# A decoder trunk of two layers: the first FFN begins on half of its first channel block, and layer 0's scale and gate come in groups of 512 channels

## The chip, the core and the metric

The kernel runs on one NeuronCore of a Trainium2 chip. The metric is the device time of one execution in microseconds (us). The engines are PE (matmul), with PEld for its weight loads, DVE (vector), ACT (scalar), POOL and SP; SP issues nearly all the DMA loads here.

## The reference

One sequence of 256 tokens and 2048 channels passes two layers in float32. Layer 0 mixes by causal pooling over 2, 4, 8 and 16 tokens in four channel groups of 512, layer 1 by latent attention; each has a SwiGLU FFN of 5632 channels behind its mixer. A condition vector c gives, by one large matrix, shift, scale and gate for each part. The change touches layer 0 up to the start of its FFN:

```python
sc = silu(c)
shift_m, scale_m, gate_m, shift_f, scale_f, gate_f = split(sc @ mod_w[0] + mod_b[0], 6)   # 2048 x 12288
h = rmsnorm(x, norm_mix) * (1 + scale_m) + shift_m
y = pool_mixer(h, pool_w, pool_scale)     # per group g of 512 channels: window means - h, then @ pool_w[g]
x = x + gate_m * y
h = rmsnorm(x, norm_ffn) * (1 + scale_f) + shift_f
x = x + gate_f * ((silu(h @ w_gate) * (h @ w_up)) @ w_down)
```

## The kernel before

**Work and precision.** FFN products are made as three passes of rounded float32: a weight tile `raw` is split into an upper part (ACT) and a lower part (DVE), and so is the activation; a block of 512 x 512 weights for 256 tokens is 24 matmuls of 128x512 (line 422 at the helper `proj_unit`). The four 512-channel blocks of the FFN's input are called j = 0 to 3. `start_ffn` takes six of the eleven chunks of 512 hidden channels (`begun`), gate and up, through j = 0, 1, 2 before the normal FFN code goes on.

**The opening** is written in a fixed order (`manual_schedule`): each engine carries out its instructions as the program lists them. A list `units` names one load of 1 MB each, and `then(n, f)` hangs other work behind unit n. Loads use six buffers (`raw`), so SP issues a load when a buffer has come free.

- `shift`, `scale`, `gate`, 16 units each, and `block`, 8 units, are `Strips`: PE multiplies each loaded tile by a column of silu(c), four narrow products (line 258), and sums in one bank. At the end `columns` copies the bank (ACT and DVE, 264 and 265), and PE turns it (269) into columns of one value a channel. `block` holds the FFN's shift and scale for j = 0.
- Seven tiles of `gate` are summed on DVE instead (241, 243).
- `Part` (213) is the other way to sum, used for the later background loads: DVE multiplies a tile of the transposed matrix by a row of silu(c) and sums along it.
- For each group g: `pool_half` (two halves: transposes 1029 and window means 1022, 1023, 1034, 1035 on PE), `pool_modulate` (four scaled shift rows on ACT, 1046, then four operations on DVE, 1048), `pool_product` (four steps of four matmuls, 1059; copy on ACT, 1062), `mix_in` (gate and residual on DVE, 1069; squares on ACT, 1073 and 1076; their sum on DVE, 1077), `turn_back` (transposes 1102, copies 1103).
- At the end: `norm_sums` (1089), a power on POOL, `norm_spread` (1110, copied at 1111), `hidden_T` (1121), and `halves_T` (1134, 1138, 1144), which gives the FFN's first input. The first FFN weights are `Halved`: two loads of half a MB.

Of the kernel before, what the change touches and what calls it, by code (L numbers as in the profile page):

```python
# [50 lines left out]
C_PAIR = C_SEL + NSTRIP  # L51
C_SHORT = C_PAIR + 2
# [8 lines left out]
TURNED_BY_DMA = (range(6, 9), range(10))  # L61

# [13 lines left out]
def shape_constants():  # L76
# [8 lines left out]
    for i in range(NSTRIP):  # L85
        con[i * STRIP, C_SEL + i] = 1.0
        con[i * STRIP, C_PAIR + i % 2] = 1.0

# [7 lines left out]
def tile_trunk(ctx: ExitStack, tc: tile.TileContext, a: dict, out: bass.AP):  # L96
# [50 lines left out]
    def load_ahead():  # L147
        kt = len(ahead)
        ahead.append(raw_t([P, 1, NSTRIP, CH]))
        sync.dma_start(ahead[kt].rearrange("p k i n -> p (k i n)"), a["mod_w"][0, kt * P:(kt + 1) * P, :D])  # L150
# [21 lines left out]
    one_strip = const.tile([P, STRIP], F32, name="one_strip")  # L172
# [6 lines left out]
    pool.memset(one_strip, 0.0)  # L179
    pool.memset(one_strip[:, 0:1], 1.0)  # L180
# [40 lines left out]
    class Strips:  # L221
        def __init__(self, i, pair, done, aside=()):
            self.aside, self.acc, self.bank = aside, None, None
            self.n, self.rows, self.done, self.kt = (2, 2, done, 0) if pair else (NSTRIP, 1, done, 0)
            self.w = a["mod_block"] if pair else a["mod_w"][0][:, i * D:(i + 1) * D].rearrange("(k p) n -> k p n", p=P)
# [9 lines left out]
        def use(self, r):  # L235
            last = self.kt + self.rows == KD
            if self.kt in self.aside:
                s_ = s_col[:, self.kt:self.kt + 1]
                if self.acc is None:
                    self.acc = gate_t([P, 1, NSTRIP, CH])  # L240
                    dve.tensor_scalar(out=self.acc, in0=r, scalar1=s_, scalar2=None, op0=ALU.mult)
                else:
                    dve.scalar_tensor_tensor(out=self.acc, in0=r, scalar=s_, in1=self.acc, op0=ALU.mult, op1=ALU.add)
            else:
                self.sum(lambda k: s_strip[:, self.kt + k, :], r, last and self.acc is None)
            if last and self.acc is not None:
                self.sum(lambda k: one_strip, self.acc, True)
            self.kt += self.rows
            if self.kt == KD:
                self.done(self.columns())  # L250

        def sum(self, weights, r, last):
            first = self.bank is None
            if first:
                self.bank = ps_t()
            for m in range(NSTRIP):
                k, i = m // self.n, m % self.n
                pe.matmul(self.bank[m * STRIP:(m + 1) * STRIP, :], lhsT=weights(k), rhs=r[:, k, i, :], start=first, stop=last)  # L258

        def columns(self):  # L260
# [5 lines left out]
            pick = con[:, C_SEL:C_SEL + NSTRIP] if self.rows == 1 else con[:, C_PAIR:C_PAIR + 2]  # L266
# [125 lines left out]
    class Halved:  # L392


        def __init__(self, src):
            shape = [P, KL, CH]
            self.src, self.raw, self.hi, self.lo = src, raw_t(shape), hl_t(shape), hl_t(shape)
            early[repr(src)] = self.hi, self.lo

        def load(self, h):  # L400
            ks = slice(h * KL // 2, (h + 1) * KL // 2)
            sync.dma_start(self.raw[:, ks].rearrange("p k n -> p (k n)"), self.src[:, ks.start * CH:ks.stop * CH])

        def upper(self, h):
            ks = slice(h * KL // 2, (h + 1) * KL // 2)
            act.activation(self.hi[:, ks], self.raw[:, ks], AF.Copy)

        def lower(self, h):
            ks = slice(h * KL // 2, (h + 1) * KL // 2)
# [1393 lines left out]
```

## Time and profile before

| | us |
|---|---|
| median of 3 runs | 1886.86 (1886.29 to 1887.82) |
| profiled execution | 1886.89 |
| its span | 1885.1 |
| PE busy | 1836.3 |
| DVE busy | 1434.9 |
| ACT busy | 836.4 |

The profiled execution stands 1.79 us above its span, which lies around the work that the profile covers. Its mean granted clock was 0.989. PE is busy at 90% or more in all slices of 47 us but the first three and the last, and a PE that is busy in the profile is not always at its peak. The DMA engines moved 592 MB, and in the first six slices they were busy all the time.

### The profile page before, as it was taken

What the parts mean: (1) busy time and instruction counts of PE and PEld (TensorE: products, weight loads), DVE (VectorE), ACT (ScalarE), POOL (GpSimd) and SP (SyncE); (2) the same over time, 40 slices, a digit from 0 to 9 for tenths busy, and PEclk for the clock granted to TensorE, in tenths of its full rate; (3) what the DMA queues carried; (4) which work ended last, traced back from release to release, by engine and by line L of the source; (5) the groups of instructions that cost most, each with busy time, mean ns of one, the idle gap of its engine ahead of it and who ended that gap; (6) DMA issues with size and microseconds to landing.
All of it is one profiled execution on the core that took longest, in us unless ns stands there. A gap on an engine that the chain in (4) does not pass through costs nothing.

```text
span 1885.1 us, 21743 instructions
## 1 busy us (share of the span) xinstructions
PE 1836.3 (97%) x8605; PEld 1488.5 (79%) x8605; DVE 1434.9 (76%) x1443; ACT 836.4 (44%) x914; POOL 68.1 (4%) x100
## 2 busy tenths in 40 slices
PE   6689999999999999999999999999999999999998
PEld 2356888888888888888889888888888888888886
DVE  1247799999889798997798886889897666645557
ACT  3125643444433344244766645643454433343343
POOL 0000000000000000000100000100011000000000
PEclk8889999999999999999999999999999999999999
DMA  9999998889999899995594485999798676776651
GB/s 399 415 420 413 386 368 331 320 313 366 407 352 419 350 403 393 386 420 217 188 379 171 160 353 189 407 358 356 279 343 320 261 261 243 260 261 234 222 201 45
DMA packets 85335, 592.27 MB, mean 314 GB/s; under 512 B 10049, under 2 KB 10481, under 8 KB 16497
## 3 DMA queue, kind: packets, MB, share of 16 engines
q1 hardware_dynamic: 79346, 570.68, 77.9%
q0 software_dynamic: 5648, 19.93, 2.9%
q8 instruction: 67, 1.10, 0.2%
q10 hardware_dynamic: 240, 0.29, 0.0%
q14 instruction: 34, 0.28, 0.0%
HBM read 576.15 MB, written 14.70 MB: 313 GB/s over the span
## 4 chain that ended last, share of the span: by engine, by line
PE 94%; DMA 5%; DVE 0%; ACT 0%; SPq 0%; issue 0%; POOLq 0%; DVEq 0%; ACTq 0%
PE ps L422 80%; DMA raw<-in_mod_w_dram 4%; PE ps L431 2%; PE ps L1059 2%; PE ps L258 2%; PE ps L1412 1%; PE ps L1498 1%; PE ps L1604 1%; PE ps L1315 1%; PE ps L807 0%; DMA raw<-in_mod_block_dram 0%; PE ps L1501 0%; PE ps L198 0%; PE ps L1513 0%; PE ps L1553 0%; PE ps L1514 0%
## 5 line engine op out<-in xcount | busy, mean ns | idle before, releaser
L422 PE MATMUL ps<-hl,act 128*128 128x512 f32 x6672 | 1517.7, 390 | 0.0
L422 PEld LDWEIGHTS ps<-hl,act 128*128 128x128 f32 x6672 | 1251.3, 188 | 259.6 <-ACT act L1134 0.8
L376 ACT ACTIVATE hl<-raw 128x2048 fp32r<-128x2048 f32 x285 | 545.9, 1918 | 631.7 <-PE ps L422 413.4
L378 DVE TENSOR_TENSOR hl<-raw,hl 128x2048 fp32r<-128x2048 f32 x285 | 651.8, 2288 | 203.6 <-ACT hl L376 203.2
L213 DVE SCALAR_TENSOR_TENSOR raw<-raw,s_row 128x2048 f32<-128x2048 f32 x168 | 383.4, 2286 | 9.9 <-DMA raw<-in_mod_wt_dram 9.9
L258 PE MATMUL ps<-raw,s_strip 128*32 128x512 f32 x392 | 59.6, 699 | 35.1 <-DMA raw<-in_mod_w_dram 34.3
L755 DVE TENSOR_TENSOR act<-ps,act 128x512 f32<-128x512 f32 x96 | 64.2, 685 | 10.3 <-PE ps L422 10.2
L258 PEld LDWEIGHTS ps<-raw,s_strip 128*32 128x32 f32 x392 | 9.2, 117 | 64.5 <-DMA raw<-in_mod_w_dram 41.6
L431 PE MATMUL ps<-hl,act 128*128 128x512 f32 x192 | 47.7, 401 | 0.6 <-DVE act L527 0.5
L431 PEld LDWEIGHTS ps<-hl,act 128*128 128x128 f32 x192 | 35.1, 188 | 10.3 <-ACT act L514 2.5
L575 POOL DMA_DIRECT2D turned<-t2k x32 | 17.8, 555 | 637.6 <-DVE t2k L573 637.4
L820 DVE TENSOR_TENSOR x<-ps,x 128x512 f32<-128x512 f32 x32 | 21.7, 691 | 20.8 <-PE ps L422 20.8
L544 DVE TENSOR_TENSOR hl<-raw,hl 128x2048 fp32r<-128x2048 f32 (+3 forms) x17 | 31.9, 1879 | 4.8 <-ACT hl L541 4.7
L265 DVE COPY t2k<-ps 128x256 f32<-128x256 f32 x4 | 1.7, 425 | 42.6 <-ACT t2k L264 42.6
L1059 PEld LDWEIGHTS ps<-act,act 128*128 128x128 f32 x128 | 24.5, 198 | 11.5 <-issue 8.4
L882 ACT ACTIVATE t2k<-ps 128x512 f32<-128x512 f32 x24 | 14.2, 592 | 42.8 <-PE ps L422 42.6
L451 ACT ACTIVATE junk<-x 128x512 bf16<-128x512 f32 x23 | 14.5, 628 | 42.1 <-DVE x L669 24.9
L753 ACT ACTIVATE act<-ps 128x512 f32<-128x512 f32 x32 | 19.0, 594 | 29.4 <-PE ps L422 29.4
L886 DVE TENSOR_TENSOR t2k<-ps,t2k 128x512 f32<-128x512 f32 x24 | 16.5, 686 | 20.1 <-PE ps L422 20.1
L1059 PE MATMUL ps<-act,act 128*128 128x256 f32 x128 | 31.7, 400 | 0.0
L541 ACT ACTIVATE hl<-raw 128x2048 fp32r<-128x2048 f32 (+1 forms) x15 | 26.5, 1766 | 3.5 <-PE ps L422 3.5
L1024 DVE COPY hl<-ps 128x256 f32<-128x256 f32 x4 | 1.7, 423 | 32.3 <-PE ps L1023 32.3
(239 smaller groups left out, 1057.2 us busy)
## 6 DMA issues: line engine op xcount, KB each, us to landing
raw<-in_mod_wt_dram SPq DMA_DIRECT2D x136, 1024.0 KB, 6.8
raw<-in_ffn_up_dram SPq DMA_DIRECT2D x88, 1024.0 KB, 6.4
raw<-in_ffn_down_dram SPq DMA_DIRECT2D x88, 1024.0 KB, 6.5
raw<-in_ffn_gate_dram SPq DMA_DIRECT2D x87, 1024.0 KB, 6.5
raw<-in_mod_w_dram SPq DMA_DIRECT2D x48, 1024.0 KB, 13.6
raw<-in_kv_mod_wt_dram SPq DMA_DIRECT2D x32, 1024.0 KB, 9.3
raw<-in_w_o_dram SPq DMA_DIRECT2D x16, 1024.0 KB, 6.6
raw<-in_mod_block_dram SPq DMA_DIRECT2D x8, 1024.0 KB, 12.5
```

Of the source, the lines that this page charges most:

```text
L213: dve.scalar_tensor_tensor(out=r, in0=r, scalar=1.0, in1=s_row, op0=ALU.mult, op1=ALU.mult, accum_out=self.sums[:, self.n:self.n + 1])
L258: pe.matmul(self.bank[m * STRIP:(m + 1) * STRIP, :], lhsT=weights(k), rhs=r[:, k, i, :], start=first, stop=last)
L376: hi_ins = act.activation(hi, r, AF.Copy)
L378: lo_ins = dve.tensor_tensor(out=lo, in0=r, in1=hi.bitcast(F32), op=ALU.subtract)
L422: pe.matmul(banks[tok], lhsT=t_[:, i, k, tok * P:(tok + 1) * P], rhs=w[:, k, :], start=first and n < len(part), stop=last and n >= len(ord ...
L431: pe.matmul(bank, lhsT=t_[:, i, k, tok * P:(tok + 1) * P], rhs=w[:, k, :], start=first and n == 0, stop=last and n == len(order) - 1)
L541: hid_ins[0] = act.activation(w[1], w[0], AF.Copy)
L544: dve.tensor_tensor(out=w[2][:, ks], in0=w[0][:, ks], in1=w[1][:, ks].bitcast(F32), op=ALU.subtract)
L753: act.activation(part, banks[tok], AF.Copy)
L755: dve.tensor_tensor(out=part, in0=banks[tok], in1=part, op=ALU.add)
L820: dve.tensor_tensor(out=sums, in0=bank, in1=sums, op=ALU.add)
L1059: pe.matmul(mixed[g][:, n % 2, :], lhsT=wp[g][:, k, ns], rhs=pool_all[g // 2][:, g % 2, k, :], start=k == 0, stop=k == KL - 1)
```

## The change

Four things are changed in the opening.

1. `scale` (called AM) and `gate` (GM) are loaded by groups of 512 channels, four units a group. Of the eight groups four stay on PE as `Strips` (`BY_PE`: scale 0 and 2, gate 0 and 3), with tiles cut by group; the other four are `Part` on DVE. The sums aside on DVE are gone.
2. Each group's pool work follows its own scale group, and its `mix_in` its own gate group. `mix_in` adds each square to the sum at once; the squares of the last group go to PE as sums of their own.
3. `block` holds the FFN's shift and scale of 256 channels only, four units. Those of the other 256 (`upper_block`) are four `Part` tiles after the first products.
4. The first two chunks of the FFN, gate and up, take j = 0 in two halves of 256 channels (`Pair`, `HalfBlock`), each load of 1 MB with gate and up side by side. The first halves of both pairs are loaded inside the last gate group. In `start_ffn` these two chunks are left out at j = 0, and the background loads begin one block later.

```diff
+AM, GM = 1, 2
+BY_PE = ((AM, 0), (AM, 2), (GM, 0), (GM, 3))
+PAIRS = 2
...
+    def group_of(m, g):
+        kt = slice(g * KL, (g + 1) * KL)
+        dst, factor = scales[m]
+        if (m, g) in BY_PE:
+            return Strips(a["mod_groups"][BY_PE.index((m, g))], 1, lambda v: add_bias(dst, v[:, 0, :], m, kt, factor))
+        return Part(a["mod_wt"][0], range(m * KD + kt.start, m * KD + kt.stop),
+                    lambda sums: add_bias(dst, sums, m, kt, factor))
...
+    block = Strips(a["mod_block"], 1, lambda v: block_cols(v[:, 0, :], 0))
+    upper_block = Part(a["mod_wt"][0], [i * KD + k for i in (3, 4) for k in range(KL // 2, KL)],
+                       lambda sums: block_cols(sums, 1))
...
-            if g + h2 == 0:
-                act.activation(squares, pair, AF.Square)
+            sq = t2k([P, 2, T])
+            act.activation(sq, pair, AF.Square)
+            if g == ND - 1 or not squares:
+                squares.append(sq)
             else:
-                sq = t2k([P, 2, T])
-                act.activation(sq, pair, AF.Square)
-                late.append(lambda sq=sq: dve.tensor_tensor(out=squares, in0=squares, in1=sq, op=ALU.add))
-                if len(late) > 1:
-                    late.pop(0)()
+                dve.tensor_tensor(out=squares[0], in0=squares[0], in1=sq, op=ALU.add)
...
-    units = [shift] * KD + [scale] * KD + [gate] * KD + [block] * (KD // 2)
-    n_mix, n_block = 2 * KD, 3 * KD
+    units = [shift] * KD + [p for m in (AM, GM) for g in range(ND) for p in [group_of(m, g)] * KL] + [block] * KL
+    n_am, n_gm, n_block = KD, 2 * KD, 3 * KD
...
     for g in range(ND):
-        then(n_mix - 8 + 2 * g, load_pool_w, g)
-        then(n_mix - 1 + 3 * g - (g > 0), pool_modulate, g)
-        for q in range(4):
-            then(n_mix + 1 + 4 * g + q, pool_product, g, q)
-    for n, f, *args in ((-1, mix_in, 0), (-1, mix_in, 1), (0, turn_back, 0), (0, mix_in, 2), (1, turn_back, 1),
-                        (1, mix_in, 3), (1, square_sums), (2, turn_back, 2), (4, norm_sums),
-                        (4, first_weights, 0), (5, norm_spread),
-                        (5, lambda: first.append(hidden_T(0)))):
-        then(n_block + n, f, *args)
+        then(n_am - 2 + KL * g, load_pool_w, g)
+        then(n_am + KL * (g + 1) - 1, pool_modulate, g)
+        for q in range(KL):
+            then(n_am + KL * (g + 1) + q, pool_product, g, q)
+        then(n_gm + KL * (g + 1) - 1, mix_in, g)
+    for g in range(ND - 1):
+        then(n_gm + KL * (g + 1) + 1, turn_back, g)
+    for c in range(PAIRS):
+        then(n_block - 5 + 2 * c, load_pair, c)
+        then(n_block - 4 + 2 * c, lambda c=c: pairs[c].split())
+    then(n_block, norm_sums)
+    then(n_block + 1, norm_spread)
+    then(n_block + 1, parts_of_first)
+    then(n_block + 2, turn_back, ND - 1)
...
-        first_weights(1)
-        turn_back(ND - 1)
-        first = halves_T(0, first[0])
-        run(copies)
-        halved[0].lower(1)
+        begun = begin(0, range(BEGUN), (0,))
...
+        near, far = (HalfBlock(t_, parts, h) for h in range(2))
+        near.upper(act)
+        near.whole(dve)
+        near.lower()
+        pairs[0].products(begun[0], t_)
+        for _ in range(KL):
+            upper_block.unit()
+        pairs[1].products(begun[1], t_)
+        later = [Pair(c, 1) for c in range(PAIRS)]
+        far.upper(dve)
+        act.activation(later[0].hi, later[0].raw, AF.Copy)
+        far.whole(act)
+        later[0].split_lower()
+        far.lower()
+        later[0].products(begun[0], t_)
+        act.activation(later[1].hi, later[1].raw, AF.Copy)
+        later[1].split_lower()
+        later[1].products(begun[1], t_)
```

How this stands on the engines is shown at three places. In the rows, `act_111` and `act_114` hold a pooled group, `hl_109` the rows of window sums, `cols` and `gm_col` the scale and gate columns, `s_row` and `s_col` silu(c).

DVE, from a scale group's column to the next group's sums. Before (modulations of groups 2 and 3 between the gate tiles that are summed aside):

```order
L243 SCALAR_TENSOR_TENSOR gate_561<-raw_606,s_col,gate_561 128x2048
L1048 SCALAR_TENSOR_TENSOR act_114<-act_114,cols,t2k_614 128x256
L1048 SCALAR_TENSOR_TENSOR act_114<-act_114,cols,t2k_617 128x256
L1048 SCALAR_TENSOR_TENSOR act_114<-act_114,cols,t2k_620 128x256
L1048 SCALAR_TENSOR_TENSOR act_114<-act_114,cols,t2k_623 128x256
L243 SCALAR_TENSOR_TENSOR gate_561<-raw_637,s_col,gate_561 128x2048
```

DVE at the same groups now (scale group 2 from PE, its modulation, then the four tiles of scale group 3):

```order
L251 COPY t2k_559<-ps_499 128x256
L955 TENSOR_TENSOR cols<-ps_562,bcol 128x4
L957 TENSOR_TENSOR cols<-cols,vcol 128x4
L1031 SCALAR_TENSOR_TENSOR act_111<-act_111,cols,t2k_586 128x256
L1031 SCALAR_TENSOR_TENSOR act_111<-act_111,cols,t2k_589 128x256
L1031 SCALAR_TENSOR_TENSOR act_111<-act_111,cols,t2k_592 128x256
L1031 SCALAR_TENSOR_TENSOR act_111<-act_111,cols,t2k_595 128x256
L214 SCALAR_TENSOR_TENSOR raw_599,sums_598<-raw_599,s_row 128x2048
L214 SCALAR_TENSOR_TENSOR raw_607,sums_598<-raw_607,s_row 128x2048
L214 SCALAR_TENSOR_TENSOR raw_615,sums_598<-raw_615,s_row 128x2048
L214 SCALAR_TENSOR_TENSOR raw_623,sums_598<-raw_623,s_row 128x2048
```

Four tiles in a row now follow a modulation that needs a column from PE and shift rows from ACT.

ACT, the shift rows of group 2. Before:

```order
L1062 ACTIVATE act_67<-ps_570 128x512
L1062 ACTIVATE act_67<-ps_601 128x512
L1046 ACTIVATE t2k_614<-hl_112,cols 128x256
L1046 ACTIVATE t2k_617<-hl_112,cols 128x256
L1046 ACTIVATE t2k_620<-hl_112,cols 128x256
L1046 ACTIVATE t2k_623<-hl_112,cols 128x256
```

ACT now:

```order
L1045 ACTIVATE act_67<-ps_524 128x512
L250 ACTIVATE t2k_559<-ps_499 128x256
L1013 ACTIVATE x<-ps_569 128x512
L1019 ACTIVATE act_111<-ps_575 128x512
L1045 ACTIVATE act_67<-ps_546 128x512
L1029 ACTIVATE t2k_586<-hl_109,cols 128x256
L1029 ACTIVATE t2k_589<-hl_109,cols 128x256
L1029 ACTIVATE t2k_592<-hl_109,cols 128x256
L1029 ACTIVATE t2k_595<-hl_109,cols 128x256
```

Ahead of the shift rows now stand the copy of the column, the last pool half's copies and the copy of the last product of group 1.

PE, the last third of the gate. Before (strips of the gate between products of group 2 and 3, all scale columns known):

```order
L258 MATMUL ps_565<-raw_676,s_strip 32x512 x4
L1059 MATMUL ps_682<-act_114,act_515 128x256 x8
L258 MATMUL ps_565<-raw_695,s_strip 32x512 x4
L1059 MATMUL ps_701<-act_114,act_515 128x256 x8
L258 MATMUL ps_565<-raw_714,s_strip 32x512 x4
L1059 MATMUL ps_720<-act_114,act_529 128x256 x4
```

PE now, at gate group 0 with the products of group 3:

```order
L1042 MATMUL ps_618<-act_111,act_473 128x256 x8
L240 MATMUL ps_647<-raw_645,s_strip 32x512 x4
L1042 MATMUL ps_652<-act_111,act_551 128x256 x4
L240 MATMUL ps_647<-raw_657,s_strip 32x512 x4
L1042 MATMUL ps_652<-act_111,act_551 128x256 x4
L240 MATMUL ps_647<-raw_668,s_strip 32x512 x4
L1042 MATMUL ps_674<-act_111,act_551 128x256 x4
L240 MATMUL ps_647<-raw_679,s_strip 32x512 x4
L255 MATMUL ps_688<-con,t2k_685 128x1 x4
L1042 MATMUL ps_674<-act_111,act_551 128x256 x4
```

The strips of a gate group now stand between products that need the modulation of the group before it, and the group's column (255) closes four units later.

More of the change, by code (lines that the diff above doesn't have):

```diff
@@ L235, in use @@
         def use(self, r):
[L236 to L253, printed above, removed]
+            first, last = self.kt == 0, self.kt + self.rows == KD
             if first:
@@ L257, in sum @@
                 k, i = m // self.n, m % self.n
-                pe.matmul(self.bank[m * STRIP:(m + 1) * STRIP, :], lhsT=weights(k), rhs=r[:, k, i, :], start=first, stop=last)
+                pe.matmul(self.bank[m * STRIP:(m + 1) * STRIP, :], lhsT=s_strip[:, self.kt + k, :], rhs=r[:, k, i, :],
+                          start=first, stop=last)
+            self.kt += self.rows
+            if last:
+                self.done(self.columns())
         def columns(self):
@@ L390, in w_unit, with proj_unit @@
         return split(r, shape)
[L392 to L409, printed above, removed]
-            dve.tensor_tensor(out=self.lo[:, ks], in0=self.raw[:, ks], in1=self.hi[:, ks].bitcast(F32), op=ALU.subtract)
-    def proj_unit(banks, t_, hi, lo, first, last, toks=range(NT), halved=False, between=None):
-        half = KL // 2
-        parts = ((hi, 0, 0, KL), (lo, 0, 0, half), (hi, 1, 0, KL), (lo, 0, half, KL)) if halved else \
-            ((hi, 0, 0, KL), (hi, 1, 0, KL), (lo, 0, 0, KL))
+    def proj_unit(banks, t_, hi, lo, first, last, toks=range(NT), between=None):
+        parts = ((hi, 0), (hi, 1), (lo, 0))
         for part in [[tok] for tok in toks] if last else [toks]:
-            order = [(w, i, k, tok) for w, i, k0, k1 in parts for k in range(k0, k1) for tok in part]
+            order = [(w, i, k, tok) for w, i in parts for k in range(KL) for tok in part]
             for n, (w, i, k, tok) in enumerate(order):
@@ new lines, in tile_trunk, with __init__, split, split_lower @@
+    class Pair:
+        def __init__(self, c, h):
+            shape = [P, 2, KL // 2, CH]
+            self.c, self.h, self.raw, self.hi, self.lo = c, h, raw_t(shape), hl_t(shape), hl_t(shape)
+            sync.dma_start(self.raw.rearrange("p w k n -> p (w k n)"), a["ffn_first"][c, h])
+        def split(self):
+            act.activation(self.hi, self.raw, AF.Copy)
+            self.split_lower()
+        def split_lower(self):
+            for w in range(2):
+                mod_ins[0] = dve.tensor_tensor(out=self.lo[:, w], in0=self.raw[:, w], in1=self.hi[:, w].bitcast(F32),
+                                               op=ALU.subtract)
+        def products(self, both, t_):
+            parts, ks, whiches, toks = ((self.hi, 0), (self.lo, 0), (self.hi, 1)), range(KL // 2), range(2), range(NT)
+            held, first, last = both[0].held, self.h == 0, self.h == 1
+            if held or first:
+                order = [(w, i, k, which, tok) for w, i in parts for k in ks for which in whiches for tok in toks]
+            else:
+                order = [(w, i, k, which, tok) for which in whiches for tok in toks for w, i in parts for k in ks]
+            seen = {}
+            for w, i, k, which, tok in order:
+                seen[which, tok] = n = seen.get((which, tok), 0) + 1
+                pe.matmul(both[which].banks[tok], lhsT=t_[:, i, self.h * len(ks) + k, tok * P:(tok + 1) * P],
+                          rhs=w[:, which, k, :], start=first and n == 1,
+                          stop=last and not held and n == len(parts) * len(ks))
```

143 lines of the change are left out of this document (80 added, 63 removed).

## The prediction

> **What bounds the kernel now.** I read the page first, then the chain of waits up to the first FFN, then the timeline of the opening, then its stretches with their granted clock.
>
> ```profile
> span 1885.1 us, 21743 instructions
> PE 1836.3 (97%) x8605; PEld 1488.5 (79%) x8605; DVE 1434.9 (76%) x1443; ACT 836.4 (44%) x914; POOL 68.1 (4%) x100
> PE   6689999999999999999999999999999999999998
> DMA  9999998889999899995594485999798676776651
> 155.01 7.84 DMA raw<-in_mod_block_dram
> 162.90 1.11 PE ps L258 x8
> 164.52 1.06 PE ps L269 x8
> 166.55 218.02 PE ps L422 x960
> 385.44 10.93 PE ps L422 x48
> ```
>
> PE is busy for 97% of the span, and its idle time (1885.1 - 1836.3 = 48.8 us) lies almost wholly in the first slices. From 166.55 on the chain is one stretch of FFN products (L422): 48 of them take 10.93 us, so one block (24 products) takes 5.46 us. Whatever moves the start of that stretch, or opens a gap in it, moves the end by as much. Before it the chain waits for a load: the last piece of `block` lands at about 162.85, and 3.7 us later the first product runs. So the opening is bound by loads, and the change asks for fewer bytes ahead of the first product. The question is whether the other engines keep up with the loads in the new order.
>
> ```profile
> 50.23 1.07 PE L258 MATMUL ps<-raw,s_strip 128*32 128x512 f32 x8 [1.43 <-DMA raw<-in_mod_w_dram]
> 101.78 1.94 PE L258 MATMUL ps<-raw,s_strip 128*32 128x512 f32 x8 [3.92 <-DMA raw<-in_mod_w_dram]
> ```
>
> These are the last tiles of shift and of scale, both taken as they landed; between them lie 16 tiles and 4 loads of the pool's weights: (101.78 - 50.23) / 20 = 2.58 us for each MB.
>
> **The change part by part.** Bytes ahead of the first product: `block` gives up 4 MB, the half MB of the first weights goes, and two loads of 1 MB (`Pair`) come: 2.5 MB less, 6.45 us, if loads stay the bound.
>
> Eight of the 16 scale tiles and eight of the 16 gate tiles go from PE strips to `Part`, a product with a sum on DVE. Before, DVE had seven gate tiles, at a time with little else to do. What this costs depends on what stands around them in DVE's order.
>
> ```profile
> 43.74 0.70 PE L1022 MATMUL ps<-hl,ones 128*128 128x256 f32 x2
> 46.34 1.07 PE L258 MATMUL ps<-raw,s_strip 128*32 128x512 f32 x8
> 52.72 0.64 PE L1029 MATMUL ps<-con,act 128*128 128x128 f32 x4
> 54.60 1.07 PE L258 MATMUL ps<-raw,s_strip 128*32 128x512 f32 x8
> 118.39 1.06 PE L258 MATMUL ps<-raw,s_strip 128*32 128x512 f32 x8
> 118.50 0.60 ACT L1062 ACTIVATE act<-ps 128x512 f32<-128x512 f32 x1 [4.05 <-PE ps L1059]
> 118.99 1.70 ACT L1046 ACTIVATE t2k<-hl,cols 128x256 f32<-128x256 f32 x4
> 119.52 1.68 DVE L1048 SCALAR_TENSOR_TENSOR act<-act,cols,t2k 128x256 f32<-128x256 f32 x4 [2.86 <-ACT t2k L1046]
> 123.04 1.07 PE L258 MATMUL ps<-raw,s_strip 128*32 128x512 f32 x8
> 236.93 2.29 DVE L213 SCALAR_TENSOR_TENSOR raw<-raw,s_row 128x2048 f32<-128x2048 f32 x1
> 239.14 0.09 DVE L213 DVE_READ_ACCUMULATOR raw<-raw,s_row 128x1 f32 x1
> ```
>
> Prices: the first half of a pool group costs PE 46.34 - 43.74 = 2.6 us, the second 1.9. A strip with two pool products takes 123.04 - 118.39 = 4.65 us; with 1.0 for the strip, a product is 1.83. DVE needs 2.21 us for a `Part` tile (to 239.14). The rows at 118.50 show the wait that matters: a copy on ACT (now L1045), behind it the four shift rows that `pool_modulate` needs (now L1029), and DVE idle for 2.86 us; from that copy's start to the end of the modulation, 2.7 us.
>
> Step 1, scale group 2. Its last tile is load 32 where before's last scale tile was load 36: it lands at 101.78 - 4 x 2.58 = 91.5, and the group's first tile at 81.2. From there PE has in order: a strip, a pool half (2.6), then three times a product and a strip (8.5): the last strip ends at 93.3. Then columns (2.7 from the strip's start, by 162.90 to 165.58 above), the second pool half (1.9) and a product (1.8): 98.7. The copy of that product stands on ACT ahead of group 2's shift rows, so the modulation ends at 98.7 + 2.7 = 101.4. All this time the four `Part` tiles of group 3 stand behind it on DVE, the first landed since 94.
>
> Step 2. Four `Part` tiles (8.8), two short operations (0.4), modulation of group 3 (1.7): 112.3. PE's products of group 3 wait for it, and the strips of gate group 0 stand between them: 0.5 for the first product's rest, three strips, two products, columns: 121.1; gate column ready at 121.5. Its last tile landed at about 112.
>
> ```profile
> 145.22 0.42 DVE L265 COPY t2k<-ps 128x256 f32<-128x256 f32 x1 [8.62 <-ACT t2k L264]
> 146.77 2.46 DVE L1069 SCALAR_TENSOR_TENSOR x<-act,gm_col,x 128x256 f32<-128x256 f32 x6
> 149.20 0.69 DVE L1077 TENSOR_TENSOR t2k<-t2k,t2k 128x512 f32<-128x512 f32 x1
> 149.33 0.63 ACT L1076 ACTIVATE t2k<-x 128x512 f32<-128x512 f32 x1 [0.16 <-DVE x L1069]
> 149.81 0.87 DVE L1069 SCALAR_TENSOR_TENSOR x<-act,gm_col,x 128x256 f32<-128x256 f32 x2
> 168.51 1.90 ACT L376 ACTIVATE hl<-raw 128x2048 fp32r<-128x2048 f32 x1
> 169.22 1.22 DVE L410 TENSOR_TENSOR hl<-raw,hl 128x1024 fp32r<-128x1024 f32 x1
> ```
>
> Step 3, DVE without a pause. A half of `mix_in` is two operations (0.82), the square on ACT (0.63, some 0.1 to start), and the sum (0.61); before, the sum was put off by one square, now DVE waits for each: 2.2, a group 4.4, group 0 (one sum only) 3.0. From 121.5: mix 0 to 124.5, four tiles and their column 133.8, mix 1 138.2, four tiles and column 147.4, mix 2 151.8. The splits of the pairs stand behind that on both engines: ACT 1.9 from 151.2, DVE 2.4, to 155.5; ACT two copies and 1.9, DVE 2.4, to 158.5. The last gate tile, which could land at 162.85 - 6.45 - 4 x 2.58 = 146.1, has its column (1.55, from 145.22 to 146.77) at 160.0.
>
> ```profile
> 157.80 1.05 PE L1089 MATMUL ps<-ones,t2k 128*128 128x1 f32 x8
> 160.40 0.70 PE L1110 MATMUL ps<-t2k,ones 128*128 128x256 f32 x2 [0.55 <-DVE t2k L1093]
> 177.97 2.10 DVE L1124 TENSOR_TENSOR t2k<-x,krT 128x256 f32<-128x256 f32 x6
> 165.45 1.07 PE L1102 MATMUL ps<-con,x 128*128 128x128 f32 x8
> 170.32 1.05 ACT L1103 ACTIVATE act<-ps 128x512 f32<-128x512 f32 x2
> raw<-in_w_kr_dram SPq DMA_DIRECT2D x1, 1024.0 KB, 4.7
> ```
>
> Step 4, the tail. Mix 3 on DVE 1.65 and the last square 0.7: 162.4. From the sums on PE to the end of the spread matmul took 160.40 + 0.70 - 157.80 = 3.3: 165.7. Behind it on PE stand a strip, eight transposes and the last strip (1.0 each); the last starts at 167.8, and the first product comes 3.65 later (162.90 to 166.55): 171.45, 4.9 us later than before. The eight more products of the three square sums lie beside mix 3. SP waits as well: the last two `block` tiles go into the buffers of the two pairs, free at 155.5 and 158.5; a load alone takes 4.7 us, so they land by 164 and are covered by steps 3 and 4.
>
> Step 5, behind the first product. PE has 48 products, 10.93. DVE needs 1.6 for the lower halves (four operations of 0.41, as in `mix_in`), 8.8 for the four tiles of `upper_block`, 0.6 to the first far channel: 11.1, so PE waits 0.2. Eight products later (1.8) it wants the lower weights, which DVE has after 0.4 + 2.4: two partial waits, 0.6 in all. DVE then carries twelve hidden pieces (0.35 each) and the splits of chunk 2: about 0.5 more for its second block. Together 1.3, from 0 to 3. The later work is the same products in another order, and PE stays the bound there: nothing.
>
> **Clock.** The sum so far is 4.9 + 1.3 = 6.2 us at full clock.
>
> ```profile
> 106.86 1.93 PE L258 MATMUL ps<-raw,s_strip 128*32 128x512 f32 x8 [0.77 <-DMA raw<-in_mod_w_dram]
> 98.60:102.00 3.40, 0.22 (x4) 0.20 (x8) 0.00 (x0) 0.00 (x0) 0.00 (x0) 0.90 1.02 422
> 102.00:105.40 3.40, 2.90 (x14) 1.18 (x6) 0.42 (x1) 1.62 (x5) 0.00 (x0) 0.50 1.01 419
> 105.40:108.80 3.40, 2.63 (x13) 0.91 (x12) 2.52 (x7) 2.06 (x5) 0.00 (x0) 0.50 1.03 424
> 108.80:112.20 3.40, 3.40 (x10) 2.79 (x11) 3.40 (x6) 0.00 (x0) 0.00 (x0) 0.60 1.00 414
> ```
>
> In these stretches (busy time of PE, PEld, DVE, ACT, POOL, then clock, DMA share, GB/s) PE fell idle, the clock was at 0.50 from 102, and it came back during the stretch from 108.80, some 5 us after the strip at 106.86, with which dense work began. The strip at 101.78 took 1.94 instead of 1.07. In the new order PE has almost nothing from 124 to 158 but four strips and some transposes, so the tail begins at half clock: 0.4 on the column, 0.9 on the first `block` strip, and about 1.0 on each sum until the clock is back 5 us after dense work begins near 160. I take 2.8 us; no effect (0) and 2.4 more, for 5 us of products at half rate, are the ends.
>
> The Trainium skill ("TensorE: Matmul & The Clock Gate", Part 1: The HAM clock gate) says that the clock halves after an idle window of about 3.4 us and returns after one such window of sustained work. The trace agrees on the halving; on the return it shows about 5 us. By the page the term would be an estimated 2.2 instead of 2.8.
>
> That a ready `Part` can't pass a waiting modulation I take from the trace: at 165.45 the last transposes were done by 166.5, but their copy ran on ACT at 170.32, behind other work that stood ahead of it in the program. The same page (Part 1, on queue depths) calls ACT and DVE strict FIFO, which speaks against this change as written; the trace agrees for ACT.
>
> Sum: 1886.89 (the profiled execution, 0.03 from the median of 1886.86) + 6.2 + 2.8 = 1895.9, say 1896.
>
> **The rivals.** (a) Loads stay the bound, the change does what it says: 2.5 MB less and the waits of step 5: 1886.89 - 6.45 + 1.3 = 1881.7, faster. For it speaks a DMA busy in every slice of the opening; against it that DVE's order ends at 158.5 what the loads allow near 149. It decides from the point where DVE has split both pairs by about 149. (b) Part of the lag is taken back, because my PE work in step 1 or the landings are too late by some microseconds: each microsecond there counts once, and 5 to 9 of them bring 1887 to 1891, no change that can be told. (c) The clock never drops: 1893.1. (d) It stays down into the products: 1898.3.
>
> **How the numbers follow.** My forecast (clock half, then back) 0.38, (c) 0.25, (d) 0.15, (a) 0.10, (b) 0.12. What a measurement of this kernel tells from no change is about 0.2%, 3.8 us: 1883.1 to 1890.6. So faster 0.10, same 0.12, slower 0.78. The forecast's own range is 1892 to 1900. The range for 8 in 10 takes in (c), (d) with the far end of step 5, and most of (b): 1888 to 1902.
>
> **What the new profile would show.** Step 1: DVE idle for over 10 us ahead of the modulation of group 2, released by ACT. Step 2: the strips of gate group 0 well behind their landing, and a second idle time of DVE of about 9 us at the gate's column. Step 3: DVE close to full from there to the splits; loads waiting for buffers, DMA below its full share. Step 4: first product near 174, at full or half clock by its stretch. Step 5: gaps in PE after the first 48 products, small. If the first product stands near 160, rival (a) is right and steps 1 to 3 are wrong; if DVE's idle times are there but the first product is on time, a price of mine is too high.

## The result and the profile after

The changed kernel is slower: 1901.47 us (median of four runs, 1898.22 to 1903.02) against 1887.34 in the runs beside it, a ratio of 1.0073 [1.0056, 1.0091]. The forecast was 1896.0 in a range of 1888 to 1902: right in direction, and about 5 us short. The result lies 0.5 us inside that range, and outside the forecast's own of 1892 to 1900. The profiled executions, 1900.38 and 1886.89, differ by 13.5, which is what the views below explain.

The page of the changed kernel, its totals and its slices:

```profile
span 1898.6 us, 21630 instructions
PE 1833.3 (97%) x8525; PEld 1494.0 (79%) x8525; DVE 1466.9 (77%) x1494; ACT 837.0 (44%) x914; POOL 67.9 (4%) x98
PE   6867999999999999999999999999999999999998
PEclk9886999999999999999999999999999999999999
DMA  9988999888999999996395394999798776776651
```

PE has 3.0 us less work than before and the span is 13.5 longer, so the loss is idle time of PE: 65.3 us instead of 48.8. In the first four slices (47 us each) PE was at 6, 6, 8 and 9 tenths, and is now at 6, 8, 6 and 7, with the clock at 6 tenths in the fourth: the second slice took work over, the third and fourth lost more.

The chain of waits through the end of the opening (start, duration, what):

```profile
159.69 2.36 DVE hl L1148 x2
162.05 0.34 DVE t2k L251
162.44 1.01 PE ps L255 x4
...
165.31 5.21 PE ps L1068 x24
...
172.39 1.15 PE ps L1083 x2
...
176.06 1.04 PE ps L240 x8
...
179.63 11.18 PE ps L1161 x48
190.83 11.42 PE ps L1161 x48
```

The first product, 166.55 before, now starts at 179.63: 13.08 of the 13.5 us have come by then. No load stands in these rows. The chain comes from DVE (the split of a pair, L1148), passes the last gate column (L251, L255) and is PE alone up to 177.1: strips, sums (L1068), spread (L1083), transposes. Its last 2.5 us are the short steps of one column (copy, bias, first channel). Behind it the 96 products of the first halves run without a gap.

### The profile page after: what moved, and what is told of

Its sections match the earlier page's. It is cut to its first block, busy times and chain, and to the rows that moved or that the text cites. A ratio compares the mean times of both kernels' runs of the same rounds, so it can differ in the third digit from the quotient of the medians.

```text
span 1898.6 us, 21630 instructions
## 1 busy us (share of the span) xinstructions
PE 1833.3 (97%) x8525; PEld 1494.0 (79%) x8525; DVE 1466.9 (77%) x1494; ACT 837.0 (44%) x914; POOL 67.9 (4%) x98
## 4 chain that ended last, share of the span: by engine, by line
PE 94%; DMA 3%; DVE 2%; ACT 1%; issue 0%; SPq 0%; POOLq 0%; DVEq 0%; ACTq 0%
PE ps L386 79%; DMA raw<-in_mod_shift_dram 2%; PE ps L395 2%; PE ps L1042 2%; PE ps L1453 1%; PE ps L1161 1%; PE ps L240 1%; DVE raw L214 1%; PE ps L1539 1%; PE ps L1645 1%; PE ps L1356 1%; PE ps L770 0%; PE ps L1542 0%; PE ps L1554 0%; PE ps L1594 0%
## 5 line engine op out<-in xcount | busy, mean ns | idle before, releaser
L386 PE MATMUL ps<-hl,act 128*128 128x512 f32 x6576 | 1495.7, 390 | 0.0
L386 PEld LDWEIGHTS ps<-hl,act 128*128 128x128 f32 x6576 | 1233.8, 188 | 255.1 <-ACT act L773 0.2
L362 ACT ACTIVATE hl<-raw 128x2048 fp32r<-128x2048 f32 x282 | 540.1, 1918 | 624.2 <-PE ps L386 396.5
L364 DVE TENSOR_TENSOR hl<-raw,hl 128x2048 fp32r<-128x2048 f32 x282 | 645.1, 2288 | 195.9 <-ACT hl L362 195.4
L214 DVE SCALAR_TENSOR_TENSOR raw<-raw,s_row 128x2048 f32<-128x2048 f32 x188 | 428.3, 2287 | 10.4 <-DMA raw<-in_mod_wt_dram 10.3
L240 PE MATMUL ps<-raw,s_strip 128*32 128x512 f32 x288 | 48.3, 764 | 28.1 <-DMA raw<-in_mod_shift_dram 22.8
L718 DVE TENSOR_TENSOR act<-ps,act 128x512 f32<-128x512 f32 x96 | 64.2, 685 | 10.2 <-PE ps L386 10.1
L395 PE MATMUL ps<-hl,act 128*128 128x512 f32 x192 | 47.6, 401 | 0.6 <-DVE act L491 0.5
L240 PEld LDWEIGHTS ps<-raw,s_strip 128*32 128x32 f32 x288 | 7.0, 123 | 51.8 <-DMA raw<-in_mod_shift_dram 23.7
L395 PEld LDWEIGHTS ps<-hl,act 128*128 128x128 f32 x192 | 35.1, 188 | 10.3 <-ACT act L478 2.5
L783 DVE TENSOR_TENSOR x<-ps,x 128x512 f32<-128x512 f32 x32 | 21.6, 691 | 19.9 <-PE ps L386 19.9
L849 DVE TENSOR_TENSOR t2k<-ps,t2k 128x512 f32<-128x512 f32 x24 | 16.5, 689 | 21.7 <-PE ps L386 21.6
L718 DVE TENSOR_TENSOR gate<-ps,gate 128x512 f32<-128x512 f32 x24 | 16.4, 685 | 11.9 <-PE ps L386 11.9
L1453 PE MATMUL ps<-act,hl 128*128 128x256 f32 x192 | 24.5, 285 | 0.0
```

The lines of the kernel that those rows point to most:

```text
L214: dve.scalar_tensor_tensor(out=r, in0=r, scalar=1.0, in1=s_row, op0=ALU.mult, op1=ALU.mult, accum_out=self.sums[:, self.n:self.n + 1])
L240: pe.matmul(self.bank[m * STRIP:(m + 1) * STRIP, :], lhsT=s_strip[:, self.kt + k, :], rhs=r[:, k, i, :], start=first, stop=last)
L362: hi_ins = act.activation(hi, r, AF.Copy)
L364: lo_ins = dve.tensor_tensor(out=lo, in0=r, in1=hi.bitcast(F32), op=ALU.subtract)
L386: pe.matmul(banks[tok], lhsT=t_[:, i, k, tok * P:(tok + 1) * P], rhs=w[:, k, :], start=first and n < len(part), stop=last and n >= len(ord ...
L395: pe.matmul(bank, lhsT=t_[:, i, k, tok * P:(tok + 1) * P], rhs=w[:, k, :], start=first and n == 0, stop=last and n == len(order) - 1)
```

## Where it was lost

The timeline from scale group 2 to that column. Last come the duration, the instruction, and in brackets the idle time ahead of it with what ended it:

```profile
95.28 0.42 DVE L251 COPY t2k<-ps 128x256 f32<-128x256 f32 x1 [10.01 <-ACT t2k L250]
...
100.96 1.68 DVE L1031 SCALAR_TENSOR_TENSOR act<-act,cols,t2k 128x256 f32<-128x256 f32 x4 [4.20 <-ACT t2k L1029]
...
112.00 1.67 DVE L1031 SCALAR_TENSOR_TENSOR act<-act,cols,t2k 128x256 f32<-128x256 f32 x4
112.58 3.25 PE L1042 MATMUL ps<-act,act 128*128 128x256 f32 x8 [2.89 <-issue]
115.76 1.41 PE L240 MATMUL ps<-raw,s_strip 128*32 128x512 f32 x8
117.10 1.99 PE L1042 MATMUL ps<-act,act 128*128 128x256 f32 x8
119.03 1.06 PE L240 MATMUL ps<-raw,s_strip 128*32 128x512 f32 x8
...
123.49 0.42 DVE L251 COPY t2k<-ps 128x256 f32<-128x256 f32 x1 [9.83 <-ACT t2k L250]
...
125.01 1.67 DVE L1052 SCALAR_TENSOR_TENSOR x<-act,gm_col,x 128x256 f32<-128x256 f32 x4
...
163.49 0.16 DVE L955 TENSOR_TENSOR gm_col<-ps,bcol 128x4 f32<-128x4 f32 x1 [1.10 <-PE ps L255]
```

DVE stands idle for 10.01, 4.20 and 9.83 us, twice for a column from PE and once for shift rows on ACT, while `Part` tiles stand behind the waiting instruction. By issue and time to landing, the last three tiles of scale group 3 had landed at 96.4, 99.0 and 101.4, so the first idle time holds up little of itself; yet DVE was done with the four only at 111.48. The last three of gate group 1 landed at 118.9, 121.3 and 124.7, and DVE began with the group at 128.05. After that it has almost no slack. The last gate column is there at 163.49; in the kernel before:

```profile
146.35 0.17 DVE L983 TENSOR_TENSOR gm_col<-ps,bcol 128x16 f32<-128x16 f32 x1 [0.70 <-PE ps L269]
```

Stretches of 3.4 us (busy time of PE, PEld, DVE, ACT, POOL, then clock, DMA share, GB/s), and SP's queue waits up to 200 us (total, count, longest):

```profile
112.20:115.60 3.40, 3.02 (x8) 2.12 (x8) 1.47 (x4) 0.00 (x0) 0.00 (x0) 0.63 0.99 395
...
142.80:146.20 3.40, 1.94 (x8) 0.23 (x8) 3.40 (x3) 0.00 (x0) 0.00 (x0) 0.50 0.22 70
...
163.20:166.60 3.40, 3.40 (x17) 1.72 (x16) 2.00 (x6) 1.26 (x2) 0.00 (x0) 0.50 0.88 311
166.60:170.00 3.40, 3.40 (x18) 3.40 (x17) 0.00 (x0) 0.00 (x0) 0.00 (x0) 0.50 1.00 414
170.00:173.40 3.40, 3.40 (x13) 1.14 (x13) 0.64 (x3) 0.00 (x0) 0.70 (x1) 0.50 1.01 422
173.40:176.80 3.40, 3.40 (x25) 1.22 (x24) 1.66 (x4) 1.47 (x3) 0.00 (x0) 0.83 1.00 419
```

```profile
SPq L213 <- PE ps L240: 35.1, 10, 6.7
...
SPq L228 <- DVE raw L214: 27.0, 6, 9.6
SPq L213 <- DVE raw L214: 22.0, 7, 7.0
```

In the second row DVE is full (3.40), PE has eight matmuls, and the DMA share is down to 0.22, because SP waits for buffers that `Part` (L214) still holds. (Over the 200 us its waits for strips on PE, L240, come to more: 64.4 us against 49.0.) The last four rows are the tail: PE busy throughout, at half clock for over 10 us.

## The experiments

The theory on record was: DVE, in order, is the late engine, because columns from PE and shift rows from ACT stand ahead of its tiles. The rivals: the clock, the square sums on PE, and the smaller first FFN itself. In the table, "column" is the start of the bias add on `gm_col` for the last gate column, "product" that of the first FFN product, both in the profiled execution. The changed kernel's four runs spread over 4.8 us, so the gains of 2 to 3 us against it (experiments 3 and 11) don't stand clear in the medians; they are read from the columns and products.

| kernel | median us | ratio to before | column | product | between |
|---|---|---|---|---|---|
| before | 1887.34 | | 146.35 | 166.55 | 20.2 |
| after | 1901.47 | 1.0073 [1.0056, 1.0091] | 163.49 | 179.63 | 16.1 |
| 1 all groups on PE | 1898.07 | 1.0056 [1.0044, 1.0069] | 161.15 | 177.83 | 16.7 |
| 2 products of group 3 later | 1892.55 | 1.0030 [1.0018, 1.0042] | 154.68 | 171.60 | 16.9 |
| 3 shift rows first on ACT | 1898.98 | 1.0064 [1.0052, 1.0077] | 161.27 | 177.43 | 16.2 |
| 4 PE kept warm | 1901.76 | 1.0075 [1.0063, 1.0088] | 164.64 | 177.44 | 12.8 |
| 5 = 2 + 3 + gate on PE | 1889.92 | 1.0007 [0.9998, 1.0015] | 151.43 | 167.15 | 15.7 |
| 6 square sums on DVE | 1901.12 | 1.0069 [1.0056, 1.0082] | 163.95 | 180.00 | 16.1 |
| 7 half FFN, gate as before | 1898.60 | 1.0054 [1.0041, 1.0066] | 154.78 | 177.34 | 22.6 |
| 8 = 5 + 6 | 1888.95 | 1.0007 [0.9998, 1.0016] | 151.20 | 167.74 | 16.5 |
| 9 = 5 + pairs behind | 1885.51 | 0.9990 [0.9981, 0.9999] | 148.04 | 164.56 | 16.5 |
| 10 = 7 + pairs behind | 1891.59 | 1.0022 [1.0013, 1.0031] | 145.96 | 167.55 | 21.6 |
| 11 after + pairs behind | 1899.07 | 1.0061 [1.0049, 1.0074] | 161.43 | 178.07 | 16.6 |
| 12 = 9 + a later turn | 1888.08 | 1.0004 [0.9995, 1.0013] | 146.36 | 164.69 | 18.3 |

**1. All eight groups as `Strips`.** `BY_PE` takes all of (AM, g) and (GM, g).

> All eight groups of scale and gate are summed by PE strips, none by `Part` on DVE; the bytes, their order, the half first FFN and `upper_block` stay as changed. If DVE's order is the cause (the `Part` tiles behind modulations and mixes), both idle times of 10 us on DVE lose their price, loads are the bound again, and the first product comes 6.45 us (2.5 MB) before that of the kernel before, at 160 to 163, with a time of 1880 to 1885 us. If the half first FFN itself is the cost (two pairs, half blocks), the first product stays behind 170 and the time above 1893. If only the cold clock costs, it goes with the denser PE, and the time is 1895 to 1897.

A miss: 3 us faster than the change, not 15 to 20. It came out as the text's second case has it (product behind 170, time above 1893), in which the half first FFN itself is the cost; experiments 7 and 10 take that up. One stretch of its opening:

```profile
120.00:130.00 10.00, 9.50 (x55) 5.41 (x55) 1.46 (x4) 1.50 (x4) 0.00 (x0) 1.00 0.88 315
```

With no tile of scale or gate on DVE, PE is the full one (9.50 of 10) and the column comes at 161.15. So what DVE has to do is not the whole cause. What I took both kernels to share is a product of the pool that waits for a modulation and stands ahead of gate tiles in PE's order; experiment 2 tests it in the changed kernel only.

**2. The products of group 3 four units later.** They now stand behind the strips of gate group 0.

```diff
-            then(n_am + KL * (g + 1) + q, pool_product, g, q)
+            then(n_am + KL * (g + 1) + q + (KL if g == ND - 1 else 0), pool_product, g, q)
```

> The four products of pool group 3 stand four units later, behind the strips of gate group 0 instead of between them; nothing else moves. By the theory of DVE's order the strips then run as their tiles land, the column of gate group 0 is ready at about 115.5 instead of 125.0 (DVE gets to it behind the modulation of group 3, at 113.7), and all behind it comes up to 9.5 us earlier: first product near 170, time 1890 to 1893. If loads or their buffers are the bound, the time stays within 3 us of the changed kernel's 1901. If the second idle time of DVE is slack, no change.

A hit, at 1892.55: 9 us from one line of order. The first gate column in its timeline:

```profile
114.68 0.42 DVE L251 COPY t2k<-ps 128x256 f32<-128x256 f32 x1 [1.01 <-ACT t2k L250]
```

DVE's idle time at the first gate column has gone from 9.83 to 1.01, and the last column is 8.8 earlier. Step 2's mechanism is shown: the order of PE's program.

**3. Shift rows ahead of the product's copy on ACT.** `pool_modulate` is registered ahead of `pool_product`.

> On ACT the four shift rows of a modulation are put ahead of the copy of the last product of the group before; nothing else moves. By the theory the modulation of group 2 then starts with its column at 96.8 instead of 100.96, the four `Part` tiles behind it come 4 us earlier (their loads have landed from 94 on), and the time falls by about 4 us to 1897. If the wait at ACT is hidden by the loads of those tiles, the time stays at 1901.

2.5 us, not 4; column and product are each 2.2 earlier. The rows of ACT and DVE:

```profile
97.70 0.60 ACT L1019 ACTIVATE act<-ps 128x512 f32<-128x512 f32 x1 [0.71 <-PE ps L1018]
98.20 1.70 ACT L1029 ACTIVATE t2k<-hl,cols 128x256 f32<-128x256 f32 x4
98.73 1.68 DVE L1031 SCALAR_TENSOR_TENSOR act<-act,cols,t2k 128x256 f32<-128x256 f32 x4 [2.47 <-ACT t2k L1029]
```

The modulation starts at 98.73 instead of 100.96. DVE's wait shrinks from 4.20 to 2.47 only, because the pool half's copy (L1019) still stands ahead of the shift rows.

**4. PE kept warm.** 36 products of the ones matrix, in five places among the gate units (37 to 46); nobody reads their bank.

```diff
+    then(45, warm, 4)
...
+    for n, m in ((37, 20), (41, 4), (44, 6), (46, 2)):
+        then(n, warm, m)
```

> The changed kernel with 36 products more, of `ones` by a tile in memory, put where PE is idle between 127 and 158; their results are used by nothing. If the half clock is paid for on the path, it is the surcharge of the rows of the chain from 163.45 to 177: (1.86 - 1.0) twice, half of 5.21, half of 1.15 and 0.5 on a strip, 5.4 us together, so 1896; by the term of the prediction 2.8, so 1898.5; if the clock is not on the path, 1901 or more, by what the added products push back.

No gain in the time. Rows of its timeline, and stretches:

```profile
165.53 3.11 PE L1068 MATMUL ps<-ones,t2k 128*128 128x1 f32 x24
...
177.44 23.66 PE L1161 MATMUL ps<-hl,act 128*128 128x512 f32 x96 [0.95 <-ACT act L1129]
```

```profile
163.20:166.60 3.40, 3.19 (x24) 2.17 (x24) 2.63 (x8) 0.59 (x1) 0.00 (x0) 1.00 1.01 427
166.60:170.00 3.40, 3.31 (x24) 2.06 (x24) 0.62 (x4) 0.67 (x2) 0.70 (x1) 0.80 1.01 422
170.00:173.40 3.40, 3.40 (x20) 1.34 (x17) 1.43 (x5) 0.38 (x1) 0.00 (x0) 0.70 1.01 424
180.20:183.60 3.40, 3.40 (x12) 2.69 (x11) 3.40 (x5) 1.91 (x1) 0.00 (x0) 0.69 0.66 202
```

The sums take 3.11 instead of 5.28, and from column to product it is 12.8 instead of 16.1. That is the price of the cold clock in the tail: 3.3 us, or more, for the clock was not full here either. The column is 1.15 later, the clock falls to 0.80 and 0.70 in the tail, and again in the products, which take 23.66 instead of 22.62. The product is 2.19 earlier and the products 1.04 longer; the 1.15 that are left don't show in the medians.

**5. Gate on PE, with both edits of order (2 and 3).** `BY_PE = ((AM, 0), (AM, 2), (GM, 0), (GM, 1), (GM, 2), (GM, 3))`.

> The two orders of the earlier experiments together (products of group 3 late, shift rows first on ACT), and all four gate groups on PE, so that DVE sums only scale groups 1 and 3. The theory as it stands after the first four runs has two parts: DVE's order delays the last gate column, and the chain of small steps behind that column (mix, sums, spread, hidden block, block column, 21 us from the last gate strip to the first product at half clock) is no longer covered, since only four `block` tiles (10.3 us) follow. Then the last gate strip runs near 147, as loads allow, and the first product comes 16 to 21 us later, at 163 to 168: 1883 to 1889 us. If the first part were all of it, the first product would follow the loads at 160, and the time would be 1881. If neither holds, the time stays at 1892 or above.

```profile
146.87 2.36 DVE L1148 TENSOR_TENSOR hl<-raw,hl 128x1024 fp32r<-128x1024 f32 x2 [1.89 <-ACT hl L1143]
148.01 1.75 PE L240 MATMUL ps<-raw,s_strip 128*32 128x512 f32 x8 [0.55 <-DMA raw<-in_mod_groups_dram]
```

```profile
166.60:170.00 3.40, 2.85 (x7) 2.27 (x8) 2.79 (x5) 0.99 (x2) 0.00 (x0) 0.50 1.00 412
```

The first product came as expected (163 to 168), the time 0.9 above the expected 1883 to 1889. The timeline rows decide rival (a) of the prediction. DVE has split both pairs by 149.23, the point from which it was to give 1881.7 with the first product near 160, and the last gate strip waits for its load alone. Yet the product comes at 167.15 and the time is no better than before's. Loads set the last gate strip now, and 15.7 us of other work follow its column. The clock has a share in this: it was 0.50 in the tail and, as the stretch shows, in the first products. The 24 sums took 4.83 (3.11 in experiment 4), the 96 products 24.91 (22.62 in the changed kernel). An estimate from these numbers puts the profiled execution of 1890.26 at 1886.2 without that: level with before, and still 4.5 above 1881.7.

**6. Square sums on DVE.** `if not squares:`, so that PE sums 8 products instead of 24.

> Every square is summed on DVE, so that the norm's sums are 8 products on PE instead of 24; nothing else changes. By the theory these sums stand bare in the chain: 5.2 us for 24 become about 1.8 for 8, and one more addition on DVE (0.7) comes in front: 2 to 3 us less, 1898.5 to 1899.5. If they lie beside mix 3, as the prediction had it, the time stays at 1901.5 or rises by the addition.

```profile
168.22 0.69 DVE L1060 TENSOR_TENSOR t2k<-t2k,t2k 128x512 f32<-128x512 f32 x1 [0.76 <-ACT t2k L1056]
169.05 1.84 PE L1068 MATMUL ps<-ones,t2k 128*128 128x1 f32 x8 [3.28 <-DVE t2k L1060]
```

A miss: the time stays, which is the text's second case (the sums lie beside mix 3). The sums take 1.84 instead of 5.28, but PE waits 3.28 for the last add, and they end at 170.89 instead of 170.52: the changed form of the sums costs nothing against this one. **8, the same on top of 5**, says it again (1888.95 against 1889.92, not 2 to 3 us less; column to product 16.5 against 15.7).

> The gates on PE, both orders, and the square sums on DVE. If the chain behind the last gate column is the bound, this takes 2 to 3 us more off than the kernel with the gates on PE and both orders alone: 1881 to 1886 us. If loads are the bound there, the two are alike.

**7. The half FFN alone.** Scale and gate are loaded and summed as before, with seven gate tiles aside on DVE; `block`, `upper_block`, pairs and first products are those of the change.

> Half of the change alone: the first FFN begins on 256 channels (`Pair`, `HalfBlock`, `upper_block`, four `block` tiles), but scale and gate are loaded and summed whole, in the order and with the seven gate tiles on DVE of the kernel before. If the loss comes with the sums by groups, the gate column is ready near 147 as before, the mixes end at 158, the norm chain runs at full clock, and the first product comes at 164 to 165, bound by that chain and not by loads: 1884 to 1886 us. If the half first FFN itself costs the loss, the time is 1895 or more. If loads were the bound, 2.5 MB less would bring 1881.

A miss that felled a theory: without any of the sums by groups the kernel still loses 0.54%. (Its first 96 products took 24.18, with the clock at 0.50 in their first stretch.) The timelines of before and of this kernel at the last gate tile:

```profile
142.82 1.07 PE L258 MATMUL ps<-raw,s_strip 128*32 128x512 f32 x8
```

```profile
148.81 1.06 PE L291 MATMUL ps<-raw,s_strip 128*32 128x512 f32 x8
...
151.35 2.36 DVE L1189 TENSOR_TENSOR hl<-raw,hl 128x1024 fp32r<-128x1024 f32 x2 [9.88 <-ACT hl L1184]
153.62 0.41 DVE L229 COPY t2k<-ps 128x256 f32<-128x256 f32 x1
```

The last gate strip is 6.0 later: ahead of its load stand the loads of two pairs, 2 MB or 5.2 us by the prediction's 2.58. Then the copy of the column waits on DVE behind the split of a pair (151.35 to 153.62). New theory: the first product is the last gate column plus a chain that changes little between kernels that sum the gate alike (15.7 to 16.9 with groups, in experiments 1 to 3, 5, 6 and 8), so bytes and splits count only where they stand ahead of that column. The change takes 4.5 MB out behind the gate and puts 2 MB ahead of its end.

**9, 10, 11. Pairs loaded and split behind the last gate tile**, in 5, in 7 and in the change.

```diff
-    for c in range(PAIRS):
-        then(n_block - 5 + 2 * c, load_pair, c)
-        then(n_block - 4 + 2 * c, lambda c=c: pairs[c].split())
+    then(n_block - 1, load_pair, 0)
+    then(n_block + 1, load_pair, 1)
+    then(n_block, lambda: pairs[0].split())
...
+    then(n_block + 1, lambda: pairs[1].split())
```

(In 10 the splits come later, behind the parts of the first input and behind the first lower half.)

Kernel 9:

> The kernel with the gates on PE and both orders, and now the two pairs are loaded and split behind the last gate tile instead of ahead of it: one right behind it, one behind the second `block` tile. The theory now: what sets the first product is the last gate strip plus a chain that is about 19 us long here (148.01 to 167.15), so that bytes ahead of the last gate tile count and bytes behind it do not, up to some 19 us. The last gate strip then comes two loads (5.2 us) earlier, near 143, the first product at 162, and the time is 1882.5 to 1884.5, below the kernel before. If all bytes ahead of the first product count alike, nothing is gained: 1889. If the two splits are in the way of the norm on DVE, 1886.

Kernel 10:

> The half first FFN alone, with scale and gate whole, and the pairs loaded behind the last gate tile; one is split after the hidden block, one after the first lower halves. If the 11 us of the half first FFN alone come from where its pairs are loaded and split, the gate column is back at 147, the mixes end at 158, the first product comes at 164 to 165, and PE then waits up to 4 us for `upper_block` on DVE: 1885 to 1889 us. If the half blocks themselves cost it, 1895 or more.

Kernel 11:

> The changed kernel, in which only the loads and splits of the two pairs are put behind the last gate tile. DVE's order with the sums by groups stays, so the last gate column waits for DVE, but not for two splits (4.7 us) and two loads: it comes 5 to 6 us earlier, the first product at 174, the time 1895 to 1896.5. If the waits of the groups on DVE were all of the loss, the time would stay at 1901.

In 9 the column comes 3.4 earlier, the product 2.6, the median 4.4. Not all of the 4.4 is the edit's for certain: the 96 products end 22.74 after their start (24.91 in 5), at full clock, and two of the eleven runs of 5 took 1884.8 and 1884.9 as they were. At 1885.51 it is the one kernel ahead of before, by 0.1% with an interval that only just leaves 1.000 out. In 10 the column is back at 145.96, before's place, and the time falls by 7.0, less than expected:

```profile
167.55 13.30 PE L1202 MATMUL ps<-hl,act 128*128 128x512 f32 x48 [2.02 <-ACT act L1170]
```

```profile
166.60:170.00 3.40, 2.45 (x6) 1.97 (x7) 3.33 (x7) 3.18 (x4) 0.00 (x0) 0.50 0.07 22
```

Its first product is 1.0 later than before's although 2.5 MB less lie behind the gate, and the 48 products take 13.30 (11.18 in the changed kernel). Part of this is the clock again, 0.50 from 159.8 to 170.0, where before's stood at 1.00 from 132.6 on: PE, with less work left, was busy for 2.66 and 2.39 of 3.40 in the two stretches ahead, where before it had 3.40. The last strip, its columns and the spread took 1.93, 1.87 and 1.20 instead of 1.07, 1.06 and 0.70. With the products' 2.1 that makes an estimated 4.3 us; without them the kernel would be level with before, not ahead. So the bytes bought nothing here, but the 21.6 us are the four mixes and the tail at a partly cold clock. In 11 the edit brings 2.4 instead of 5 or more:

```profile
153.66 1.73 PE L1078 MATMUL ps<-con,x 128*128 128x128 f32 x6 [1.37 <-DVE x L1052]
155.31 3.64 PE L240 MATMUL ps<-raw,s_strip 128*32 128x512 f32 x16
```

The last two gate tiles (each is x8 in such a row) run in one go at 155.31: they stood behind the transposes of group 2, which waited for its mix on DVE. With DVE late, the loads' place matters little.

**12. In 9, the transposes of group 2 behind the last gate strips.** `turn_back` of group 2 is hung three units later.

> The kernel with the gates on PE, both orders and the pairs behind the gate, and now the transposes of group 2 (`turn_back`) stand behind the first `block` strip on PE instead of ahead of the last two gate strips. In the kernel without it these two strips run at 144.45 behind transposes that wait for mix 2 on DVE. If the last gate strip is what sets the first product, the gate column comes about 2 us earlier (DVE ends mix 2 at 145.1, so no more), the first product at 162.7, and the time is 1883 to 1884. If DVE or the loads are the bound there, the time stays at 1885.5.

```profile
153.00 2.36 DVE L1148 TENSOR_TENSOR hl<-raw,hl 128x1024 fp32r<-128x1024 f32 x2 [4.57 <-ACT hl L1143]
155.27 0.15 DVE L419 TENSOR_SCALAR sm<-ps 128x2 f32<-128x2 f32 x1
```

The column is 1.7 earlier, before's place, and the product is not: the split of a pair now holds DVE until 155.27, and the first step of the norm (L419) stands behind it. The gain became a wait a few rows on; the runs (1885.43 to 1890.08) overlap those of 9. The profiled execution is the fastest of them, so these rows don't show why the median is 2.6 above it.

## Why the prediction was right in direction and short in size

The sum was 9.0 (6.2 and 2.8 for the clock), the profiled executions differ by 13.5. The 4.5 between them are: 3.9 at the start of the last mix (163.88 for 160.0) and 1.5 behind it (15.75 from there to the first product, where step 4 has 171.45 - 160.0 = 11.45 and the clock 2.8), less 0.9 in step 5.

That the result still lies in the range for 8 in 10 is in part luck. The upper end was reached for with a clock that stays down into the products and the far end of step 5; neither came, and the room was filled by other terms that were too small.

**Step 1 held.** DVE's idle times of 10.01 and 4.20, with ACT as their releaser, are as forecast; the modulation of group 2 ends at 102.64, 1.2 later than reckoned.

**Step 2 held in its mechanism, and its last term was too small: this is the step that failed in size.** Experiment 2 shows the mechanism. The modulation of group 3 ends at 113.67 (1.4 late), but the column of group 0 is used at 125.01 (3.5 late). Of the other 2.1, the clock accounts for 1.6: at 0.63, eight products took 3.25 instead of 1.99, and a strip 1.41 instead of 1.06. I had charged the cold clock to the tail alone, although PE had stood idle here too (2.89 ahead of the products).

**Step 3 was right.** From the start of mix 0 to that of mix 3 it reckoned 38.5; measured are 38.9 (125.01 to 163.88), with the waits for buffers and the low DMA share that it named.

**Step 4 was nearly right at full clock.** Of its products of the square sums it said that the additional ones "lie beside mix 3". In experiment 4, with the sums at full clock, they do: mix 3 starts at 165.03, the last square is there at 167.43, and the sums end at 168.64, 3.6 after the start of the mix, where the step has 2.4 + 1.05. In the changed kernel, at 0.50, the same 24 take 5.28 and end 6.6 after it. Experiment 6 agrees: the other form isn't cheaper. The last term, 3.65 from the last strip to the first product, is 3.57 in the chain (176.06 to 179.63).

**The clock term was too small.** The 15.75 behind the start of the last mix are 4.3 above step 4's 11.45. Experiment 4 takes 3.3 off, although a strip (1.93) and the spread (1.22) still ran cold in it, so most of the 4.3 is clock, where the term has 2.8, with 0.4 of it ahead of the mix. Its course was off too: the clock came back after 10 us of work and not 5. It was back before the products, so rival (d) didn't come in this kernel, though the profiles of experiments 4, 5, 7 and 10 show it in part. Rival (c), no drop at all, is out by the 0.50 of the tail.

**Step 5** gave 1.3 in a range of 0 to 3 and cost 0.4 (13.5 - 13.08).

**The rivals.** Rival (a) was worked out wrongly. Experiment 5 reaches its condition and ends at 1889.92, not 1881.7. The cold clock accounts for an estimated 4.0 or more of the 8.2 us between (see there). For the rest I argue that its 6.45 us for 2.5 MB are a net of two things of unlike worth: 4.5 MB less behind the gate, where 2.5 MB less bought nothing in experiment 10, and 2 MB more ahead of its end. The trace of before had the sign of it, in PE's row for the last `block` strip:

```profile
162.90 1.07 PE L258 MATMUL ps<-raw,s_strip 128*32 128x512 f32 x8 [0.80 <-DMA raw<-in_mod_block_dram]
```

PE waited 0.80 us for that load, and no more than that could be won at this place before the work behind the gate column set the end. Taken back edit by edit, the column goes from 163.49 to 154.68 (order of the products), 151.43 (gate on PE, ACT's order), 148.04 (pairs behind) and 146.36 (transposes behind), before's 146.35. The 2 us that experiment 9 is ahead of before, less than the 3.8 that the prediction took for telling, would seem to come with the groups, not with the smaller first FFN: three mixes are done by the time of its column (16.5 to the first product), where experiment 10, with the gate whole, needs 21.6. This is argued, not shown.

Two things stay open: the sums by groups with the first FFN whole were not tried, and none of the changed kernels held full clock through tail and products, so what the change, or experiments 4, 5 and 10, would be worth without the cold clock is known by estimate only.

## What to carry to other kernels

Look for the last value that everything else hangs on (here a column of the gate), and measure the chain behind it: in these kernels saved bytes and moved sums paid little behind that value, and what was put ahead of it, on a queue or an engine that works in order, delayed it. Write consumers of late values as far back in the program as their own consumers allow; one line of order was worth 9 us here, a whole redistribution of sums between DVE and PE (experiment 1) 3. And when a wait is taken away, read what stands next on the same engine: four of the twelve edits (3, 6, 11, 12) gave all or part of their gain back there. Look at the granted clock too before a time is put down to bytes or order: work taken off PE left it colder in the tail (experiment 10).

## What the runs showed of the hardware

The granted clock stayed at 0.50 for three stretches, 10.2 us, in which the profile shows PE busy for 3.40 of 3.40 with one-column sums and narrow strips, and came back (0.83) in the fourth. In experiment 4 it fell from 1.00 to 0.80 and 0.70 in stretches with PE busy for 3.31 and 3.40. The Trainium skill ("TensorE: Matmul & The Clock Gate", Part 1: The HAM clock gate) says that the clock returns after one window of about 3.4 us of sustained work. These rows don't agree, if busy in the profile is meant: it took three times that. In the same trace the clock stood at 0.84 from 156.40 to 159.80, with PE busy for only 2.27 of 3.40, and was at 0.66 and 0.50 in the stretches behind. What the gate counts as work the runs don't tell; both spells are made of one-column sums, narrow strips and small products.
